# Router logits of a transformer block taken from the un-normed rows, with the row factor, the bias and three small pieces of work moved

## The chip, the core and the metric

The kernel runs on one NeuronCore of one Trainium2 chip. The core has five engines that run their own instruction streams and wait for one another through semaphores: PE (the matrix engine, with its weight loads shown as PEld), DVE (vector work), ACT (activations, casts, copies), POOL (general work and indirect DMA) and SP (which here only issues DMAs). Sixteen DMA engines move data between the chip's memory and the on-chip buffers; SP, ACT and POOL each have a queue that feeds them.

The metric is the device time of one execution in microseconds. The kernel before takes 1404.52 us (median of 3 runs, 1404.02 to 1405.08).

## The reference

One encoder block on a sequence of 1024 rows of width 1024, in float32. Cut to what the change touches:

```python
(shift1, scale1, gate1, shift2, scale2, gate2) = split(silu(c) @ w_ada + b_ada, 6)
...
x  = x + gate1 * (mix @ w_out)                      # mix: two groups of attention heads
h2 = rms_norm(x, norm2_g) * (1 + scale2) + shift2   # rms_norm: x * rsqrt(mean(x*x) + eps) * g
g_logits = h2 @ w_router_group + b_router_group     # 4 groups
e_logits = h2 @ w_router_expert + b_router_expert   # 32 experts, 8 to a group
# the best group; inside it the best 2 experts; weights g_prob * softmax of the two
# each chosen expert: (silu(h2 @ w_gate) * (h2 @ w_up)) @ w_down, width 512 inside
x = x + gate2 * (sum over the two experts, weighted)
return rms_norm(x, final_norm_g)
```

With r = rsqrt(mean(x*x) + eps) of a row, G2 = norm2_g * (1 + scale2) and B2 = shift2, the row is h2 = x * r * G2 + B2, and so h2 @ W + b = r * (x @ (G2 * W)) + (B2 @ W + b).

## The kernel before, in words

The program is one function, `tile_hymba`, written straight down, and a layer under it puts the recorded instructions into one stream per engine. An engine runs its stream strictly in order, so an instruction that waits holds up everything behind it on its engine.

**Stage 1** (to about 260 us) makes the vectors shift1 to gate2 from c, the normed rows, and the projections of the attention heads. Matrix products in float32 are made of three products of a high and a low part (`mm3`, lines 68 to 71). `ada_in`, `ada_add` and `ada_out` interleave the vectors gate1, shift2, scale2 and gate2 (v = 0, 1, 2, 3) with the projections: DVE sums the weighted rows of w_ada into `acc`, and `ada_out(v)` turns `acc` into a column of 128 x 8 on PE (L380), adds the bias on DVE (L382) and stores it to `ada_d` in the chip's memory. When the region of hThi and hTlo is free, SP loads the first heads (L542), and **stage 2**, the attention, follows (to about 640 us).

**Stage 3** (640 to 760 us) is where most of the change lies. It goes over eight tiles t of 128 rows. Per tile: `out_proj` on PE (the tile `pm`, two halves n of 512 columns), `residual(t, n)` on DVE (L972, L973: x2 = pm * gate1 + x) with the sum of squares on ACT, `norm2(t)` (the row factor st[:, 6:7], then h2 = x2 * factor * G2 + B2 in four DVE operations, L992 and L993), the store of h2 to `h2_d` and of x2 to `x2_d`, `flip_h2(t)` (eight transposes on PE, copied out by ACT), and `logits(t)` (eight products with the router's columns `wr`, L1016, and the bias `brt` added on DVE, L1017). The last tile, t = 7, takes its factor by a square root on ACT and a reciprocal; the others by a power on POOL and two Newton steps on DVE (`rsqrt2`).

Two sets of tiles are routed apart: tA (tiles 0 to 4) while stage 3 runs, tB (5 to 7) at its end. `choose` finds group and experts (some 24 small DVE operations), `rank` and `place` give each row its slot, `table` sums one-hot products on PE into `pid` (row numbers) and `pwt` (weights), `weigh` makes the weights in three bfloat16 parts, and `spread` multiplies them out. From `pid` comes `tg`, the table of row numbers; `gather` is an indirect DMA on POOL's queue that reads the rows of an expert from `h2_d`.

**Stage 4** (from 760 us) runs the 32 experts. `x_T` turns the gathered rows (8 transposes, a cast on ACT and a subtraction on DVE for the low part, L1437). The weights, loaded ahead into 14 buffers, are split into high and low parts by `split_e` (a cast on ACT, L1175, and a subtraction on DVE, L1176), one split per chunk of six products on PE. `chunk` asks for splits up to 5 ahead of its own, in program order, so the ten splits before `glu_up` of expert 0 stand ahead of expert 1's `x_T` on DVE. The constants SP0 and SP1 say how many splits are made before the choice and after the gather.

Of the kernel before, what the change touches and what calls it, by code (L numbers as in the profile page):

```python
# [43 lines left out]
SP0, SP1, GU0, NW, NX0 = 2, 3, 13, 14, 4  # L44
# [7 lines left out]
def tile_hymba(  # L52
# [311 lines left out]

    aps = ExitStack()
# [61 lines left out]

    wr = consts.tile([128, 8, 36], F32, name="wr")
    brt = consts.tile([128, 36], F32, name="brt")
    Y.dma_start(wr[:, :, 0:4], w_router_group[0].rearrange("(k p) n -> p k n", p=128))  # L430
    Y.dma_start(wr[:, :, 4:36], w_router_expert[0].rearrange("(k p) n -> p k n", p=128))
    Y.dma_start(brt[:, 0:4], b_router_group.to_broadcast([128, 4]))
    Y.dma_start(brt[:, 4:36], b_router_expert.to_broadcast([128, 32]))
# [531 lines left out]
    def residual(t, n):  # L965

        if n == 0:
            x2s[t] = tile_a(F32)
            sts[t] = sp.tile([128, 8], F32, name="st3", tag="st3", bufs=3)
        ns = slice(n * 512, n * 512 + 512)  # L970
        x2 = x2s[t][:, ns]
        V.tensor_mul(x2, pms[t, n], gate1[:, ns])  # L972
        V.tensor_add(x2, x2, xt3[t][:, ns])  # L973
        A.activation(xt3[t][:, ns], x2, AF.Square, accum_out=sts[t][:, n:n + 1])
        if t == NT - 1 and n == 0:
            A.activation(sts[t][:, 4:5], epsc, AF.Sqrt)
        if t == NT - 1 and n == 1:
            V.tensor_scalar(sts[t][:, 2:3], sts[t][:, 0:1], 1.0 / D, EPS, op0=ALU.mult, op1=ALU.add)
        if n == 1:
            Y.dma_start(x2_d[t * 128:(t + 1) * 128], x2s[t])  # L980

    def norm2(t):
        st = sts[t]
        if t == NT - 1:
            A.activation(st[:, 3:4], st[:, 1:2], AF.Sqrt, bias=st[:, 2:3], scale=1.0 / D)
            V.reciprocal(st[:, 6:7], st[:, 3:4])
        else:
            rsqrt2(st)
# [5 lines left out]
        Y.dma_start(h2_d[t * 128:(t + 1) * 128], h2s[t])  # L994
# [9 lines left out]
    def flip_h2(t):  # L1004
        hTs3[t] = tile_a(F32).rearrange("p (k q) -> p k q", k=8)
        for b in range(2):
            ptr = ps3.tile([128, 512], F32, name="ptr3", tag="tr")
            for i in range(4):
                j = 4 * b + i
                T.transpose(ptr[:, i * 128:(i + 1) * 128], h2s[t][:, j * 128:(j + 1) * 128], ident)  # L1010
            A.copy(hTs3[t][:, 4 * b:4 * b + 4], ptr.rearrange("p (k q) -> p k q", k=4))

    def logits(t):
# [3 lines left out]
        V.tensor_add(LG[:, t], pl[:, 0:36], brt)  # L1017
# [160 lines left out]

    LEAD, LEAD1, ES = 5, 3, 28
# [20 lines left out]
    for t in range(NT + 1):  # L1200
# [3 lines left out]
        elif t < NT:  # L1204
            if t == 3:
                flip_h2(1)
# [15 lines left out]
        if 0 < t:  # L1222
            norm2(t - 1)
        if t == NT:
            split_to(SP0)
            weigh(tA, G)
        flips = [0] if t == 2 else [t - 1] if t > 2 else []
        for u in flips:
            flip_h2(u)
# [23 lines left out]
        if t == NT - 1:  # L1253
            residual(t, 1)
# [18 lines left out]
    gather(xb0, tg[:, 0:1])  # L1273
    weigh(tB, V)
    split_to(SP1)
    table(pwt, EW, tB)
# [74 lines left out]
    def flip4(cols):  # L1351
        ptr = ps4.tile([128, 512], F32, name="ptr4", tag="tr")[:, 0:4 * C]
        for i in range(4):
            T.transpose(ptr[:, i * C:(i + 1) * C], cols[i], ident[:C, :C])  # L1354
        return ptr

    def x_cols(xb, b):

        v = xb.rearrange("c (q p j) -> c q j p", p=128, j=2)
        return [v[:, 2 * b + i // 2, i % 2] for i in range(4)]  # L1360

    def wide(t, i):

        return t[:, i * C:i * C + 128]

    def stat(pool, name, n, dtype=F32R):

        t = pool.tile([128, n * C + 128 - C], dtype, name=name) if pool else tile_a(dtype)[:, :n * C + 128 - C]
        G.memset(f32(t[:, n * C:]), 0.0)
        return t  # L1370

# [58 lines left out]
    def x_T(xb):  # L1430
        xTs.reverse()
        xT = xTs[0]
        for b in range(2):
            ptr = flip4(x_cols(xb, b))
            o = [xT[:, (8 * l + 4 * b) * C:(8 * l + 4 * b + 4) * C] for l in range(2)]
            A.copy(o[0], ptr)
            V.tensor_sub(o[1], ptr, f32(o[0]))  # L1437
        return xT

    def chunk(ps, xT, e, ch):  # L1440
# [3 lines left out]
        for k2 in range(2):  # L1444
            k = 2 * (ch % 4) + k2
            mm3(ps, wide(xT, k), wide(xT, 8 + k), hi[:, k2], lo[:, k2], k == 0, k == 7)
# [6 lines left out]
    xT = x_T(xb0)  # L1453
# [179 lines left out]
```

## Time and profile before

| what | value |
|---|---|
| runs | 1404.52 us median, 1404.02 to 1405.08 |
| the profiled execution | 1404.29 us, its span 1402.5 us |
| PE busy | 1304.8 us, 93% |
| DVE busy | 1082.4 us, 77% |
| ACT busy | 771.9 us, 55% |
| POOL busy | 537.5 us, 38% |
| DMA in all | 357.06 MB, mean 255 GB/s |

The page's strip of 40 slices (35 us each) has one hole in PE's row that this change is near:

```profile
PE   5799999887999999989995999999999989999993
...
PEclk9899999998999999999995999999999999999995
```

Each digit is a busy share in tenths, and PEclk the granted clock of PE in tenths of full speed. Slice 21 (736 to 771 us) is the hand-over from stage 3 to stage 4: PE is at five tenths there and its clock too. Span and execution differ by 1.79 us, which lies around the span.

### The profile page before, as it was taken

How to read it: one execution, taken by the hardware profiler on the slowest of the kernel's cores; microseconds unless marked ns; L12 is line 12 of the kernel's file. 1: busy time of each engine (PE TensorE's matmuls, PEld its weight loads, DVE VectorE, ACT ScalarE, POOL GpSimd, SP SyncE). 2: the span in 40 equal slices, each digit the busy share in tenths (PEclk: the TensorE clock that was granted, in tenths of full speed). 3: DMA queues.
4: the chain of work that ended last, by engine and by line, in shares of the span. 5: the costliest groups of instructions: out<-in, count | busy, mean ns of one | idle time of the engine just before them, and what ended most of it. 6: DMA issues, size and time to landing. Idle time of an engine off the chain costs nothing. (4 is left out here: it accounts for less than half of the span.)

```text
span 1402.5 us, 18267 instructions
## 1 busy us (share of the span) xinstructions
PE 1304.8 (93%) x6343; PEld 1050.9 (75%) x6343; DVE 1082.4 (77%) x1610; ACT 771.9 (55%) x1194; POOL 537.5 (38%) x361
## 2 busy tenths in 40 slices
PE   5799999887999999989995999999999989999993
PEld 4578789765888888878884777777777767777762
DVE  5887646557788888874568798888888888888876
ACT  5531224346666766661224667766666756666653
POOL 2102100047666666650002244444444532544332
PEclk9899999998999999999995999999999999999995
DMA  9528963681344525238966999999989997999946
GB/s 330 163 91 265 309 234 123 182 306 53 87 139 113 172 84 192 71 132 291 342 229 256 357 367 361 356 380 372 324 318 329 354 342 286 363 375 356 380 153 246
DMA packets 123969, 357.06 MB, mean 255 GB/s; under 512 B 15781, under 2 KB 41474, under 8 KB 122338
## 3 DMA queue, kind: packets, MB, share of 16 engines
q1 hardware_dynamic: 79794, 200.11, 41.1%
q10 hardware_dynamic: 29376, 113.25, 21.2%
q0 software_dynamic: 14704, 42.51, 10.0%
q8 instruction: 51, 0.84, 0.2%
q14 instruction: 44, 0.36, 0.1%
HBM read 306.52 MB, written 57.69 MB: 260 GB/s over the span
## 5 line engine op out<-in xcount | busy, mean ns | idle before, releaser
L1176 DVE TENSOR_TENSOR ra<-rb,ra 128x1024 fp32r<-128x1024 f32 x249 | 290.5, 1220 | 51.5 <-ACT ra L1175 47.3
L1348 POOL DMA_INDIRECT x_d<-y,tg x32 | 223.4, 6983 | 124.0 <-DVE y L1418 108.5
L1175 ACT CAST ra<-rb 128x1024 fp32r<-128x1024 f32 x249 | 242.4, 1049 | 1.9 <-PE pg L70 1.3
L626 PE MATMUL s<-ra 128*128 128x512 f32 x448 | 130.8, 409 | 5.1 <-DVE stg L592 3.1
L1176 DVE TENSOR_TENSOR ra<-rx,ra 128x1024 fp32r<-128x1024 f32 x103 | 120.5, 1217 | 17.0 <-ACT ra L1175 14.6
L647 ACT ACTIVATE e<-s,mx 128x1024 f32<-128x1024 f32 x96 | 107.5, 1120 | 38.4 <-DVE mx L642 21.5
L642 DVE TENSOR_REDUCE mx<-s 128x1 f32<-128x1024 f32 x96 | 116.7, 1217 | 12.4 <-PE s L626 12.3
L69 PE MATMUL pz<-whi,hThi 128*128 128x512 f32 (+2 forms) x320 | 118.6, 371 | 5.1 <-ACT hThi L272 5.1
L70 PE MATMUL pz<-wlo,hThi 128*128 128x512 f32 (+2 forms) x320 | 116.5, 364 | 0.4 <-DVE wlo L135 0.4
L69 PE MATMUL pg<-ra,xT 128*128 128x512 f32 x256 | 114.9, 449 | 0.1
L953 POOL DMA_INDIRECT xb<-h_d,tg x31 | 31.0, 999 | 219.1 <-PE ptr L1354 198.7
L71 PE MATMUL pz<-whi,hTlo 128*128 128x512 f32 (+2 forms) x320 | 112.8, 360 | 0.1
L70 PE MATMUL pg<-ra,xT 128*128 128x512 f32 x256 | 102.3, 400 | 6.9 <-DVE ra L1176 6.9
L658 ACT CAST rb<-ptr 128x512 fp32r<-128x512 f32 x128 | 74.3, 588 | 59.8 <-PE ptr L654 59.1
L69 PE MATMUL pu<-ra,xT 128*128 128x512 f32 x256 | 104.1, 407 | 0.0
L71 PE MATMUL pg<-ra,xT 128*128 128x512 f32 x256 | 102.9, 402 | 1.1 <-DVE xT L1437 1.1
L1175 ACT CAST ra<-rx 128x1024 fp32r<-128x1024 f32 x103 | 101.2, 1048 | 2.3 <-DVE ra L1176 1.4
L70 PE MATMUL pu<-ra,xT 128*128 128x512 f32 x256 | 101.1, 395 | 0.1
L71 PE MATMUL pu<-ra,xT 128*128 128x512 f32 x256 | 101.2, 395 | 0.0
L626 PEld LDWEIGHTS s<-ra 128*128 128x128 f32 x448 | 81.6, 191 | 22.8 <-ACT e L647 4.2
L659 DVE TENSOR_TENSOR rb<-ptr,rb 128x512 fp32r<-128x512 f32 x128 | 86.3, 680 | 9.7 <-ACT rb L658 9.5
L654 PE MATMUL ptr<-ident,e 128*128 128x128 f32 x512 | 78.0, 275 | 9.0 <-POOL e L802 5.3
(365 smaller groups left out, 3020.9 us busy)
## 6 DMA issues: line engine op xcount, KB each, us to landing
rb<-in_w_expert_up_dram ACTq DMA_DIRECT2D x26, 1024.0 KB
rb<-in_w_expert_down_dram ACTq DMA_DIRECT2D x26, 1024.0 KB
rb<-in_w_expert_gate_dram ACTq DMA_DIRECT2D x24, 1024.0 KB
rb<-in_w_expert_gate_dram SPq DMA_DIRECT2D x20, 1024.0 KB
rb<-in_w_expert_down_dram SPq DMA_DIRECT2D x20, 1024.0 KB
rb<-in_w_expert_up_dram SPq DMA_DIRECT2D x19, 1024.0 KB
aw<-in_w_ada_dram SPq DMA_DIRECT2D x32, 512.0 KB
ra<-qk_d SPq DMA_DIRECT2D x48, 256.0 KB
```

Of the source, the lines that this page charges most:

```text
L69: T.matmul(ps, ahi, bhi, start=first, stop=False)
L70: T.matmul(ps, ahi, blo, start=False, stop=False)
L71: T.matmul(ps, alo, bhi, start=False, stop=last)
L626: T.matmul(ps[:, ns], l, r[:, ns], start=i == 0, stop=i == len(parts) - 1)
L642: V.reduce_max(mx, ps, axis=AX.X, negate=True)
L647: A.activation(e, ps, AF.Exp, bias=nb, scale=1.0, accum_out=z)
L654: T.transpose(ptr[:, i * 128:(i + 1) * 128], e[:, (4 * b + i) * 128:(4 * b + i + 1) * 128], ident)
L658: A.copy(hi[:, :, q], src)
L659: return lambda: V.tensor_sub(lo[:, :, q], src, f32(hi[:, :, q]))
L1175: A.copy(hi, raw[:, 2 * half:2 * half + 2])
L1176: V.tensor_sub(lo, raw[:, 2 * half:2 * half + 2], f32(hi))
L1348: G.indirect_dma_start(out=x2_d, out_offset=bass.IndirectOffsetOnAxis(ap=si, axis=0), in_=y, in_offset=None, bounds_check=S - 1, oob_is_er ...
```

## The change

It has seven parts.

1. The router's columns and bias are loaded a few lines further up. In `ada_out(1)` the bias becomes brt + shift2 @ W (eight products of 128 x 36 on PE, one DVE addition), and in `ada_out(2)` the columns are multiplied by G2 (one small load, one transpose, two DVE operations).
2. `flip_h2` becomes `flip_x2`: it turns x2, not h2, and `logits` multiplies by the row factor as it adds the bias. For tile 7 the turn comes in two halves, each behind its half of the residual.
3. The stores of h2 are issued from POOL's queue in place of SP's.
4. `weigh(tA)` moves from behind `norm2(7)` to a place ahead of `residual(7, 0)`, and its last multiplication from POOL to DVE.
5. Tile 7 takes its factor by `rsqrt2` as the others do; its h2 is x2 * G2 made in the residual and finished by one operation of 128 x 1024 on DVE behind `choose(tB)`, stored after it.
6. SP0 goes from 2 to 1 and that split moves behind the gather; the turn of expert 0's rows moves ahead of the weights' sum and the positions, with 2 splits behind it.
7. The buffers of the gathered rows are cleared by DVE in place of POOL; the first, `xb0`, is cleared on POOL in tile 7.

```diff
-SP0, SP1, GU0, NW, NX0 = 2, 3, 13, 14, 4
+SP0, SP1, GU0, NW, NX0 = 1, 3, 13, 14, 4
...
+        if v == 1:
+            for k in range(8):
+                T.matmul(pr[:, 256:292], col[:, k:k + 1].to_broadcast([128, 128]), wr[:, k], start=k == 0, stop=k == 7)
+            V.tensor_add(brt, brt, pr[:, 256:292])
+        if v == 2:
+            n2r = ap.tile([8, 128], F32, name="n2r", tag="row8")
+            Y.dma_start(n2r, norm2_g[0].rearrange("(j p) -> j p", p=128))
+            T.transpose(pr[:, 256:264], n2r, ident[:8, :8])
+            V.scalar_tensor_tensor(col, col, 1.0, pr[:, 256:264], op0=ALU.add, op1=ALU.mult)
+            V.tensor_mul(wr, wr, col[:, :, None].to_broadcast([128, 8, 36]))
...
-        G.memset(xbufs[-1], 0.0)
+        V.memset(xbufs[-1], 0.0)
...
-        if t == NT - 1 and n == 0:
-            A.activation(sts[t][:, 4:5], epsc, AF.Sqrt)
-        if t == NT - 1 and n == 1:
-            V.tensor_scalar(sts[t][:, 2:3], sts[t][:, 0:1], 1.0 / D, EPS, op0=ALU.mult, op1=ALU.add)
+        if t == NT - 1:
+            if n == 0:
+                h2s[t] = tile_a(F32)
+            V.tensor_mul(h2s[t][:, ns], x2, G2[:, ns])
...
-        Y.dma_start(h2_d[t * 128:(t + 1) * 128], h2s[t])
+        G.dma_start(h2_d[t * 128:(t + 1) * 128], h2s[t])
...
-                T.transpose(ptr[:, i * 128:(i + 1) * 128], h2s[t][:, j * 128:(j + 1) * 128], ident)
+                T.transpose(ptr[:, i * 128:(i + 1) * 128], x2s[t][:, j * 128:(j + 1) * 128], ident)
...
-        V.tensor_add(LG[:, t], pl[:, 0:36], brt)
+        V.scalar_tensor_tensor(LG[:, t], pl[:, 0:36], sts[t][:, 6:7], brt, op0=ALU.mult, op1=ALU.add)
...
-        if 0 < t:
+        if t == NT:
+            flip_x2(t - 1, [1])
+            rsqrt2(sts[t - 1])
+        elif 0 < t:
             norm2(t - 1)
-        if t == NT:
-            split_to(SP0)
-            weigh(tA, G)
+        if t == NT - 1:
+            weigh(tA, V)
...
             if t == NT - 1:
                 load_w(GU0)
+                flip_x2(t, [0])
...
         if t == NT - 1:
+            xb0 = tile_a(F32)[:C]
+            G.memset(xb0, 0.0)
+        if t == NT - 1:
             residual(t, 1)
...
-    xb0 = tile_a(F32)[:C]
-    G.memset(xb0, 0.0)
     pid, pwt = (pmp.tile([128, 512], F32, name="pt3", tag="pm") for _ in range(2))
     table(pid, EI, tA)
-    table(pwt, EW, tA)
     choose(tB)
+    t = NT - 1
+    V.scalar_tensor_tensor(h2s[t], h2s[t], sts[t][:, 6:7], B2, op0=ALU.mult, op1=ALU.add)
+    G.dma_start(h2_d[t * 128:(t + 1) * 128], h2s[t])
     pcB = rank(tB)
...
     gather(xb0, tg[:, 0:1])
+    table(pwt, EW, tA)
     weigh(tB, V)
+    table(pwt, EW, tB)
+    split_to(SP0)
+    xT0 = [stat(None, "", 8) for l in range(2)]
+    x_turn(xb0, lambda: ps3.tile([128, 512], F32, name="ptr3", tag="tr"), lambda l, b: xT0[l][:, 4 * b * C:(4 * b + 4) * C])
     split_to(SP1)
-    table(pwt, EW, tB)
     V.tensor_copy(wt, pwt[:C, 0:NE])
...
-    xT = x_T(xb0)
+    xT = xT0
```

DVE at the end of tile 6 and in tile 7, before the change: `ra<-pm,ra` is the residual's first operation (pm is out_proj's result), `oc`, `RK` and `ra<-iot_s,RK` are `place(tA)`.

```order
L993 TENSOR_TENSOR ra<-ra,B_6106 128x512
L972 TENSOR_TENSOR ra<-pm,ra 128x512
L973 TENSOR_TENSOR ra<-ra 128x512
L1077 TENSOR_TENSOR oc<-OH,pc 128x320
L1079 TENSOR_REDUCE RK<-oc 128x10
L1081 TENSOR_TENSOR ra<-iot_s,RK 128x960
L972 TENSOR_TENSOR ra<-pm,ra 128x512
L973 TENSOR_TENSOR ra<-ra 128x512
```

The same place after the change; the rows from `w_6880` on are the end of `weigh(tA)`.

```order
L1002 TENSOR_TENSOR ra<-ra,B_6120 128x512
...
L1122 CAST w_6880<-rest 128x10
L1081 TENSOR_TENSOR ra<-OH,w_6880 128x960
L985 TENSOR_TENSOR ra<-pm,ra 128x512
L986 TENSOR_TENSOR ra<-ra 128x512
L991 TENSOR_TENSOR ra<-ra,G_6122 128x512
L1088 TENSOR_TENSOR oc<-OH,pc 128x320
L1090 TENSOR_REDUCE RK<-oc 128x10
L1092 TENSOR_TENSOR ra<-iot_s,RK 128x960
L985 TENSOR_TENSOR ra<-pm,ra 128x512
```

Between norm2(6) and residual(7, 0) now stand the ten operations of `weigh(tA)`, and a multiplication by G2 stands behind each half of the residual.

DVE from the gathered rows of expert 0 to those of expert 1, before: `xT<-ptr` is the low part of the turned rows, `ra<-rx,ra` and `ra<-rb,ra` are splits of weights, `sg<-sg,pu` is `glu_up`.

```order
L1282 COPY cnt<-pc 128x32
L1437 TENSOR_TENSOR xT_7118<-ptr_7129,xT_7118 128x384
L1437 TENSOR_TENSOR xT_7118<-ptr_7136,xT_7118 128x384
L1176 TENSOR_TENSOR ra<-rx,ra 128x1024 x5
L1176 TENSOR_TENSOR ra<-rb,ra 128x1024 x5
L1378 TENSOR_TENSOR sg<-sg,pu 96x512
L1437 TENSOR_TENSOR xT_7116<-ptr_7252,xT_7116 128x384
```

The same stretch after:

```order
L1216 TENSOR_TENSOR ra<-ptr_7088,ra 128x384
L1216 TENSOR_TENSOR ra<-ptr_7095,ra 128x384
L1187 TENSOR_TENSOR ra<-rx,ra 128x1024 x2
L1329 COPY wt<-pt_6971 96x32
...
L1334 COPY cnt<-pc 128x32
L963 MEMSET xb_7136 96x1024
L963 MEMSET xb_7138 96x1024
L1187 TENSOR_TENSOR ra<-rx,ra 128x1024 x5
L1187 TENSOR_TENSOR ra<-rb,ra 128x1024 x5
L1409 TENSOR_TENSOR sg<-sg,pu 96x512
L1216 TENSOR_TENSOR xT_7151<-ptr_7271,xT_7151 128x384
```

Two splits, the sum of the weights with the positions (`wt` to `cnt`) and two clearings now stand between the two turns; before, only the ten splits and `glu_up` did.

## Rows read from the trace of the kernel before

**Rows 1.** The page's first line.

```profile
span 1402.5 us, 18267 instructions
```

**Rows 2.** Windows: stretch, length, busy us of engines, PEclk, DMA share, GB/s.

```profile
740.00:745.00 5.00, 4.70 (x24) 4.33 (x23) 4.42 (x12) 2.46 (x3) 0.17 (x1) 0.50 1.03 421
755.00:760.00 5.00, 0.47 (x7) 0.47 (x6) 4.82 (x7) 0.00 (x0) 3.13 (x5) 0.50 0.21 63
800.00:840.00 40.00, 40.00 (x182) 31.52 (x181) 35.21 (x38) 26.31 (x34) 21.00 (x5) 1.00 1.01 368
```

**Rows 3.** Waits of PE, 770 to 1375 us: total, times, longest.

```profile
PE pg L70 <- DVE ra L1176: 6.9, 1, 6.9
```

**Rows 4.** Waits of SP's queue, 150 to 300 us.

```profile
SPq L542 <- PE pz L71: 29.4, 1, 29.4
```

**Rows 5.** Timeline of DVE, the last two tiles: start, us, operation.

```profile
730.21 0.69 DVE L993 TENSOR_TENSOR ra<-ra,B 128x512 f32<-128x512 f32 x1
731.45 0.69 DVE L972 TENSOR_TENSOR ra<-pm,ra 128x512 f32<-128x512 f32 x1 [0.55 <-PE pm L71]
...
733.82 1.16 DVE L1081 TENSOR_TENSOR ra<-iot_s,RK 128x960 bf16<-128x960 f32 x1
735.06 0.69 DVE L972 TENSOR_TENSOR ra<-pm,ra 128x512 f32<-128x512 f32 x1
```

**Rows 6.** The same: weigh(tA), first and last of nine, then the choice.

```profile
742.85 0.17 DVE L1103 TENSOR_REDUCE gs<-GE 128x5 f32<-128x20 f32 x1
...
744.52 0.18 DVE L1111 CAST w<-rest 128x10 bf16<-128x10 f32 x1
745.19 0.19 DVE L1017 TENSOR_TENSOR LG<-pl,brt 128x36 f32<-128x36 f32 x1 [0.49 <-PE pl L1016]
...
745.62 1.03 DVE L1028 TENSOR_TENSOR fk<-LG,GM 128x12 f32<-128x12 f32 x1
```

**Rows 7.** Timeline of PE, end of stage 3 to the first expert.

```profile
734.87 1.87 PE L1016 MATMUL pl<-wr,ra 128*128 128x36 f32 x16
739.42 1.09 PE L1010 MATMUL ptr<-ident,ra 128*128 128x128 f32 x4 [2.69 <-DVE ra L993]
...
741.69 3.47 PE L1016 MATMUL pl<-wr,ra 128*128 128x36 f32 x16
...
759.97 1.51 PE L1354 MATMUL ptr<-ident,ra 96*128 96x96 f32 x8
...
```

**Rows 8.** Timeline of DVE from the choice's end to expert 1's rows.

```profile
750.65 0.26 DVE L1050 TENSOR_TENSOR OB<-OH 128x96 bf16<-128x96 f32 x1
...
754.04 0.18 DVE L1272 TENSOR_TENSOR tg<-tgf,pt 96x32 int32<-96x32 f32 x1
...
755.42 2.85 DVE L1111 CAST w<-rest 128x6 bf16<-128x6 f32 x1
...
760.53 0.18 DVE L1277 COPY wt<-pt 96x32 f32<-96x32 f32 x1
...
763.04 0.18 DVE L1282 COPY cnt<-pc 128x32 f32<-128x32 f32 x1
...
764.08 5.75 DVE L1176 TENSOR_TENSOR ra<-rx,ra 128x1024 fp32r<-128x1024 f32 x5
...
778.13 1.01 DVE L1437 TENSOR_TENSOR xT<-ptr,xT 128x384 fp32r<-128x384 f32 x2
```

**Rows 9.** Timeline of POOL: the first gather and a clearing.

```profile
755.10 1.14 POOL L953 DMA_INDIRECT ra<-h_d,tg  x1 [7.59 <-DVE wts L1106]
756.25 0.97 POOL L950 MEMSET xb<- 96x1024 f32 x1
```

**Rows 10.** The tile qk_d: landing of POOL's 256 KB stores in stage 1.

```profile
DMA to landing us min/median/max: 2.3/4.1/10.1
```

**Rows 11.** The lines with DVE's clearings: durations in ns, first start, form.

```profile
L79 DVE MEMSET ones<- x1: 165/165/165, 0.9 to 0.9; 128x128 f32 x1
L81 DVE MEMSET epsc<- x1: 59/59/59, 1.0 to 1.0; 128x1 f32 x1
```

More of the change, by code (lines that the diff above doesn't have):

```diff
@@ L362, in tile_hymba @@
         V.tensor_copy(nlam, plam[:, 0:1])
+    wr = consts.tile([128, 8, 36], F32, name="wr")
+    brt = consts.tile([128, 36], F32, name="brt")
+    Y.dma_start(wr[:, :, 0:4], w_router_group[0].rearrange("(k p) n -> p k n", p=128))
+    Y.dma_start(wr[:, :, 4:36], w_router_expert[0].rearrange("(k p) n -> p k n", p=128))
+    Y.dma_start(brt[:, 0:4], b_router_group.to_broadcast([128, 4]))
+    Y.dma_start(brt[:, 4:36], b_router_expert.to_broadcast([128, 32]))
     aps = ExitStack()
@@ L425, in tile_hymba @@
                 turn_pair(rps, h, sb.tile([128, 2, 512], F32R, name="stg", tag="stg", bufs=4), hs, 2)
[L428 to L433, printed above, removed]
     iot = consts.tile([128, 48], F32, name="iot")
@@ L983, in norm2 @@
         st = sts[t]
[L984 to L988, printed above, removed]
+        rsqrt2(st)
         h2s[t] = tile_a(F32)
@@ L1002, in rsqrt2, with flip_x2 @@
         V.tensor_mul(st[:, 6:7], st[:, 5:6], st[:, 4:5])
-    def flip_h2(t):
-        hTs3[t] = tile_a(F32).rearrange("p (k q) -> p k q", k=8)
-        for b in range(2):
+    def flip_x2(t, bs=range(2)):
+        if t not in hTs3:
+            hTs3[t] = tile_a(F32).rearrange("p (k q) -> p k q", k=8)
+        for b in bs:
             ptr = ps3.tile([128, 512], F32, name="ptr3", tag="tr")
@@ L1177, in split_e, with flip4, x_cols, wide @@
         return hi, lo
+    def flip4(cols, new=None):
+        ptr = (new() if new else ps4.tile([128, 512], F32, name="ptr4", tag="tr"))[:, 0:4 * C]
+        for i in range(4):
+            T.transpose(ptr[:, i * C:(i + 1) * C], cols[i], ident[:C, :C])
+        return ptr
+    def x_cols(xb, b):
+        v = xb.rearrange("c (q p j) -> c q j p", p=128, j=2)
+        return [v[:, 2 * b + i // 2, i % 2] for i in range(4)]
+    def wide(t, i):
+        return t[:, i * C:i * C + 128]
+    def stat(pool, name, n, dtype=F32R):
+        t = pool.tile([128, n * C + 128 - C], dtype, name=name) if pool else tile_a(dtype)[:, :n * C + 128 - C]
+        G.memset(f32(t[:, n * C:]), 0.0)
+        return t
+    def x_turn(xb, new, part):
+        for b in range(2):
+            ptr = flip4(x_cols(xb, b), new)
+            A.copy(part(0, b), ptr)
+            V.tensor_sub(part(1, b), ptr, f32(part(0, b)))
     LEAD, LEAD1, ES = 5, 3, 28
@@ L1205, in tile_hymba @@
             if t == 3:
-                flip_h2(1)
+                flip_x2(1)
             if t < NT - 1:
@@ L1221, in tile_hymba @@
             load_w(GU1)
-        if 0 < t:
+        if t == NT:
+            flip_x2(t - 1, [1])
+            rsqrt2(sts[t - 1])
+        elif 0 < t:
             norm2(t - 1)
-        if t == NT:
-            split_to(SP0)
-            weigh(tA, G)
+        if t == NT - 1:
+            weigh(tA, V)
         flips = [0] if t == 2 else [t - 1] if t > 2 else []
         for u in flips:
-            flip_h2(u)
+            if t < NT:
+                flip_x2(u)
         if 0 < t < NT:
@@ L1349, in scatter @@
                              in_=y, in_offset=None, bounds_check=S - 1, oob_is_err=False, compute_op=ALU.add)
[L1351 to L1370, printed above, removed]
     def glu_gate(pg):
@@ L1432, in x_T @@
         xT = xTs[0]
[L1433 to L1438, printed above, removed]
+        x_turn(xb, None, lambda l, b: xT[:, (8 * l + 4 * b) * C:(8 * l + 4 * b + 4) * C])
+        return [xT[:, 0:8 * C + 128 - C], xT[:, 8 * C:]]
     def chunk(ps, xT, e, ch):
```

2 lines of the change are left out of this document (1 added, 1 removed).

## The prediction

> **What bounds the kernel now.** I read the span first [rows 1], then the windows by stage, then PE's waits, then the timelines of PE, DVE and POOL round the hand-over from stage 3 to the experts, because the parts of the change lie there and in stage 1. In the expert stage PE is busy in all of a 40 us window at the full clock [rows 2], and in 600 us it waits once for longer than 2.2 us, 6.9 us for a split of DVE [rows 3]. So that stage is a fixed length of PE work, and what counts is when PE gets expert 0's and expert 1's rows and whether splits arrive in time. At the hand-over PE is idle most of the time and its clock is at 0.50, 1.2 GHz, where it is at 1.00, 2.4 GHz, in the experts [rows 2]; the reader is to see DVE at 4.4 and 4.8 of 5 us there: it sets the pace. DMA is saturated at 740 to 745 and at 0.21 at 755 to 760 [rows 2]: the loads ahead are in by then.
>
> **The change, part by part.**
>
> *Stage 1.* Eight more products of PE. Eight products with the 36 columns of `wr` take 1.87 us at the full clock [rows 7]; I take 1.8. They lie on the path: SP's first loads for the attention wait for PE's last product of this stage, 29.4 us in all [rows 4], and everything later follows from those. The transpose and the three DVE operations are small beside it and DVE waits for PE there. Bounds: 0, if a later wait for something else swallows it, and 2.0.
>
> *Un-normed rows and POOL's stores, tiles 0 to 6.* PE is the busy engine until 735 us and does as many transposes and products as before; the multiplication is in the same DVE operation as the bias. SP no longer waits for h2 between its loads, but PE does not wait for those loads. The stores stand on POOL between the factors' powers, each behind the h2 of its own tile, which is finished long before the next power is asked for. I cost all this at nothing; the cover is PE's full queue, and without it each store would put its issue before a power.
>
> *weigh(tA) ahead of residual(7, 0).* DVE finishes norm2(6) at 730.21 + 0.69 = 730.90 and then waits 0.55 for PE [rows 5]: that is all the room there is. The nine small operations take 742.85 to 744.70, 1.85 us [rows 6]; the multiplication that comes over from POOL has 960 columns and I take the 1.16 of place's operation of that size [rows 5]. So residual(7, 0) starts at 733.91 and not 731.45. From there to the end of place it was 734.98 - 731.45 = 3.53, and the G2 operation adds 0.69: residual(7, 1) starts at 738.13 in place of 735.06 [rows 5], 3.1 us late.
>
> A cast of the second weigh took 2.85 us and not 0.18 [rows 6, 8], while POOL issued the gather and cleared buffers from 755.10 on [rows 9]. After the change three such casts run at 731.7 to 732.8, just when POOL issues the store of h2(6) and then clears `xb0` (0.97 [rows 9]). The stall there lies between 0 and the 1.0 of that clearing; I take 0.5. The Trainium skill, "SBUF — State Buffer", section "Who interferes with whom", says that a cast of DVE can use two ports and then shares a lock with POOL, so that whoever comes second waits for all of the other's instruction. By it the stall would be the whole 1.0 and the sum 0.5 us more. The same page warns of DMAs issued from POOL for the mirror reason; no row here has DVE's casts holding up an issue.
>
> *The last tile.* x2's second half is there 1.4 us after 738.6, at 740.0. Before, its normed rows reached PE in two parts at 739.42 and 740.8, PE's clock low after an idle of 2.69 us, and the eight products took 3.47 us from 741.69, against 1.87 at the full clock [rows 7]. Now one half is turned already; the other takes 1.09 at the low clock, the products start at about 741.0 and the logits are there at 744.55 and not 745.19 [rows 6]. The factor is ready earlier: its chain is 1.8 us behind the sum of squares. So four DVE passes saved buy only 0.65 us, since DVE came 3.6 us late. If PE held 2.4 GHz through 740 us, half of 1.09 + 3.47 would go, and the logits come at 742.3.
>
> *Choice to gather.* It was 745.19 to 754.22, 9.03 us [rows 6, 8]. One operation there took 1.03 and its neighbours 0.18, beside POOL's part of weigh, which is gone: -0.85. The last h2 operation of 128 x 1024 is inserted, 1.15 (five in 5.75 [rows 8]). Row numbers at 744.55 + 9.33 = 753.9, before 754.2. The gather started 0.9 after that [rows 9]. Now it also waits for the last store, which cannot be issued before 744.55 + (750.91 - 745.19) - 0.85 + 1.15 = 750.6. Landing: 256 KB stores of POOL took 2.3 to 10.1, median 4.1 [rows 10]; this one has 512 KB but quieter engines than at 740. I take 4.1: 754.7, and the gather at 754.8 in place of 755.10. With 2.3 the 0.9 could go too; with 10.1 the gather starts at 760.7. Expert 0's rows are turned 4.87 us behind the gather's start [rows 7, 9], so the hand-over moves by -0.3 (bounds -3 and +5.6).
>
> *Expert 0 to expert 1.* Call the start of that turn F, 759.97 before [rows 7]. Then DVE had 18.16 us until the low part of expert 1's rows at 778.13 [rows 8], and PE had finished expert 0 by then. Now DVE has, in this order: 1.5 for PE's turn [rows 7], 1.0 for two subtractions, 2.3 for two splits, 2.6 from `wt` to `cnt` (760.53 to 763.15), two clearings, 11.5 for ten splits, 0.6 for `glu_up`. For the clearings the only rows of DVE are 165 ns for 128 columns and 59 ns for one [rows 11]: 0.83 ns a column, 0.9 for 1024 columns (bounds 0.17, if the size hardly counts, and POOL's 0.97). That is F + 21.3, 3.15 late. Before, the two splits lay at 740 us, in front of the choice, the sum of the weights lay beside PE's first turn, and the clearings were POOL's. This is the largest term, and no later slack gives it back, since PE's work from expert 1 on is a fixed length. Bounds: 1.5, clearings cheap and the misses partly in DVE's own old gaps, and 4.
>
> *The clock.* PE idles some 3 us there, and after 2.69 us it was found at half clock [rows 7]. Some products at 1.2 GHz, between 0 and 2 us; I take 0.5.
>
> Sum: 1.8 - 0.3 + 3.15 + 0.5 = 5.15. Against the profiled execution's own 1404.29, which is its span and 1.79 around it and lies 0.2 below the median of the runs: 1404.29 + 5.15 = 1409.4.
>
> **Rivals.**
>
> *The clock holds.* The turn of the first half and tile 6's logits now fill PE's gap after 735 us. If that keeps PE at 2.4 GHz to the choice, the logits come at 742.3, the store is out by 748.4, and the hand-over moves by -0.3 - 2.25; expert 1 then has no clock to lose. It decides if the clock falls later than 741. For it: one gap of 2.7 us becomes two short ones. Against it: 0.50 in all of 740 to 745 [rows 2], and the second gap is still some 2 us. 1.8 - 2.55 + 3.15 = +2.4: 1406.7, not slower by what can be told.
>
> *The late work of DVE is hidden.* If ACT or the buffers hold the ten splits back, as a gap of 2 us in DVE's row between them did before, the extra 3.15 lies in time that was lost anyway. With the hand-over as in the clock's case and stage 1's products swallowed by the attention's waits: 0 - 2.55 - 0.5 (the gather earlier by most of its 0.9) = -3: 1401.3, faster. Against it: the ten splits stand behind the clearings in one stream, ACT's casts are ahead by then.
>
> *The last store is late.* The gather waits for all eight h2 stores. If POOL's store shares the engines with the last weights, it lands like the 10.1 us row, and the hand-over is 5.6 late: 1409.4 + 5.9 = 1415.3. Against it: 0.21 of DMA at 755 [rows 2].
>
> **How the numbers follow.** Forecast 0.52, the clock holds 0.22, hidden 0.14, late store 0.12. About 0.2% (2.8 us) is what a measurement of this kernel can tell from no change. The forecast's own range, 1406 to 1412, is slower by 0.2% in about nine of ten: 0.47 slower, 0.05 same. The clock's case lies on the edge: 0.17 same, 0.03 slower, 0.02 faster. Hidden: 0.09 faster, 0.05 same. Late store: slower. Together slower 0.62, same 0.27, faster 0.11. The range, with both outer cases cut to 2 in 10: 1402.5 to 1412.5.
>
> **What would show it.** In the profile after: PE's last product of stage 1 at about 1.8 us later; residual(7, 1) 3 us later than that against its old place; the logits of tile 7 near their old time; the gather waiting for a DMA or for the row numbers; DVE without a gap from expert 0's turn to expert 1's and PE waiting some 3 us at expert 1's first low-part product. I am wrong if the stage 1 shift is gone by 640 us, if PE does not wait at expert 1, or if the clock stands at 1.00 through 745 us.

## The result: 1.3% slower, most of it one gather that stood on POOL

| | median us | runs |
|---|---|---|
| before | 1404.27 | 1401.16 to 1405.08, 4 runs |
| changed | 1421.83 | 1419.98 to 1422.56, 4 runs |

The ratio is 1.0126 with a 95% interval of 1.0114 to 1.0139. The prediction said 1409.4 with a range to 1412.5: the direction was right and the size was not, 17.6 us in place of 5.

The page's first line and two rows of its strip, in the changed kernel (slices of 35.5 us):

```profile
span 1420.5 us, 18319 instructions
...
PE   5799999897999999989995699999999989999993
...
PEclk9899999999999999999996899999999999999996
```

The hole at the hand-over now spreads into the slice behind it. The windows (columns as in [rows 2]) show both halves of it, the old one at 740 to 760 us and a new one at 785 to 795, where PE is busy 1.48 of 10 us; from 800 us on PE is full again as before:

```profile
740.00:745.00 5.00, 3.10 (x24) 3.04 (x25) 4.86 (x9) 2.01 (x5) 0.00 (x0) 0.75 1.03 421
755.00:760.00 5.00, 1.51 (x16) 1.43 (x17) 3.73 (x16) 1.10 (x3) 1.52 (x2) 0.50 0.26 105
785.00:795.00 10.00, 1.48 (x8) 1.26 (x8) 0.45 (x2) 0.48 (x1) 2.50 (x3) 0.60 1.03 316
800.00:840.00 40.00, 40.00 (x182) 31.52 (x181) 32.72 (x36) 25.52 (x34) 15.70 (x4) 1.00 0.92 318
```

PE's waits from 770 to 1375 us, to be read against [rows 3], name it. The 6.9 us wait is still there; above it stands a new one for `xb`, the gathered rows of expert 1, and it is a wait for a DMA, not for DVE:

```profile
PE ptr L1193 <- DMA xb<-h_d,tg: 11.8, 1, 11.8
PE pg L70 <- DVE ra L1187: 9.5, 2, 6.9
```

POOL's timeline round the hand-over shows why the DMA was late. L966 is the gather, L1311 the store of the last h2:

```profile
755.04 0.59 POOL L1311 DMA_DIRECT2D h_d<-ra  x1 [9.09 <-DVE EM L1106]
759.07 1.08 POOL L966 DMA_INDIRECT ra<-h_d,tg  x1 [3.44 <-DVE w L1122]
...
773.82 11.88 POOL L966 DMA_INDIRECT xb<-h_d,tg  x1 [2.34 <-DVE xb L963]
785.70 0.81 POOL L1170 DMA_DIRECT2D rb<-in_w_expert_up_dram  x1
```

Expert 0's gather took 1.08 us on POOL, expert 1's 11.88. Before, the latter stood ahead of the splits:

```profile
764.00 0.99 POOL L953 DMA_INDIRECT xb<-h_d,tg  x1 [0.69 <-POOL hF L1369]
```

DVE's timeline beside it (to compare with [rows 5], [rows 6] and [rows 8]):

```profile
735.42 1.16 DVE L1122 CAST w<-wts 128x10 bf16<-128x10 f32 x1
...
738.52 0.68 DVE L985 TENSOR_TENSOR ra<-pm,ra 128x512 f32<-128x512 f32 x1
...
748.62 0.26 DVE L1028 SCALAR_TENSOR_TENSOR LG<-pl,st,brt 128x36 f32<-128x36 f32 x1 [1.99 <-PE pl L1027]
...
757.81 0.18 DVE L1319 TENSOR_TENSOR tg<-tgf,pt 96x32 int32<-96x32 f32 x1
...
772.63 0.91 DVE L963 MEMSET xb<- 96x1024 f32 x1 [0.16 <-issue]
773.47 5.69 DVE L1187 TENSOR_TENSOR ra<-rx,ra 128x1024 fp32r<-128x1024 f32 x5
779.08 5.76 DVE L1187 TENSOR_TENSOR ra<-rb,ra 128x1024 fp32r<-128x1024 f32 x5
784.76 0.68 DVE L1409 TENSOR_TENSOR sg<-sg,pu 96x512 f32<-96x512 f32 x1
794.98 1.20 DVE L1216 TENSOR_TENSOR xT<-ptr,xT 128x384 fp32r<-128x384 f32 x2 [9.55 <-ACT xT L1215]
```

The gather was asked for at 773.82, inside the first of ten splits that follow one another without a gap, and it ended at 785.70, which is 0.94 behind the start of `glu_up` at 784.76: its own work (0.96 where nothing holds it) done once the splits were over. DVE then idled 9.55 us, and PE started expert 1 at 795.00 in place of 777.97.

The hold is not all of the delay. The rows landed 19.6 us after the gather was asked for:

```profile
DMA to landing us min/median/max: 19.6/19.6/19.6
```

Of these 11.9 are POOL's, and 7.8 passed behind them, at a DMA share of 1.03 in 785 to 795. Expert 0's rows landed 3.1 us behind their gather's end, at a quieter time. How much sooner the rows would have come through free DMA engines was not tested.

Four markers cut the 18.0 us between the two spans into stretches:

| marker | before | changed | lost in the stretch |
|---|---|---|---|
| PE, last `prb` turn of the attention | 632.22 | 635.97 | 3.75 |
| PE, turn of expert 0's rows | 759.97 | 763.40 | -0.32 |
| DVE, low part of expert 1's rows | 778.13 | 794.98 | 13.42 |
| end of the span | 1402.5 | 1420.5 | 1.15 |

The first and the last line are single readings. The attention's end moves by some us among the profiles of the same stage 1 (below), and the last stretch is 623.9 to 627.7 us long in the profiles of the experiments that change nothing in it, against 624.4 before and 625.5 here.

### The profile page after: what moved, and what is told of

Read it like the earlier page. It is cut to its first block, busy times and chain, and to the rows that moved or that the text cites. A ratio compares the mean times of both kernels' runs of the same rounds, so it can differ in the third digit from the quotient of the medians.

```text
span 1420.5 us, 18319 instructions
## 1 busy us (share of the span) xinstructions
PE 1305.5 (92%) x6360; PEld 1050.5 (74%) x6360; DVE 1085.2 (76%) x1618; ACT 768.7 (54%) x1190; POOL 548.8 (39%) x369
## 5 line engine op out<-in xcount | busy, mean ns | idle before, releaser
L966 POOL DMA_INDIRECT xb<-h_d,tg x31 | 41.7, 1346 | 218.4 <-PE ptr L1193 196.4
L69 PE MATMUL pg<-ra,xT 128*128 128x512 f32 x248 | 111.0, 447 | 0.0
L70 PE MATMUL pg<-ra,xT 128*128 128x512 f32 x248 | 98.6, 398 | 6.9 <-DVE ra L1187 6.9
L69 PE MATMUL pu<-ra,xT 128*128 128x512 f32 x248 | 101.0, 407 | 0.0
L71 PE MATMUL pg<-ra,xT 128*128 128x512 f32 x248 | 98.8, 398 | 0.0
L71 PE MATMUL pu<-ra,xT 128*128 128x512 f32 x248 | 98.2, 396 | 0.0
L70 PE MATMUL pu<-ra,xT 128*128 128x512 f32 x248 | 98.0, 395 | 0.1
```

The source lines that it names most:

```text
L69: T.matmul(ps, ahi, bhi, start=first, stop=False)
L70: T.matmul(ps, ahi, blo, start=False, stop=False)
L71: T.matmul(ps, alo, bhi, start=False, stop=last)
```

## The experiments

### The gather that is held

`e1_clear_on_pool`, the clearings back on POOL:

```
-        V.memset(xbufs[-1], 0.0)
+        G.memset(xbufs[-1], 0.0)
```

> The changed kernel with one edit: the two buffers of the gathered rows are cleared by POOL again. The trace of the changed kernel has expert 1's gather on POOL for 11.88 us, from 773.82 to 785.70, beside ten splits of DVE that follow one another without a gap from 773.47 to 784.84. Theory A (DVE's run of splits keeps POOL from writing the gather's descriptors): the gather still stands on POOL behind the clearing of hF, which waits for DVE's positions, so it is asked for just when the splits begin; it starts some 2 us earlier and is again held for about 11 us, to the end of the splits. PE waits about 10 us for expert 1's rows; 1419.5 to 1420.5, some 2 us under the changed kernel. Theory B (the gather was late because it stood behind the two clearings on DVE): it takes about 1 us, its rows land before DVE has done the splits, and PE waits about 3 us; some 9 us under the changed kernel, 1412 to 1414.

Measured: 1411.50 us, 1.0048 [1.0031, 1.0065] of before, some 10 us under the changed kernel. The number is near theory B's 1412 to 1414, the trace is neither's:

```profile
772.81 0.12 POOL L1208 MEMSET hF<- 128x32 f32 x1 [0.38 <-DVE pos L1134]
773.57 1.28 POOL L966 DMA_INDIRECT xb<-h_d,tg  x1 [0.63 <-POOL hF L1208]
774.85 0.81 POOL L1170 DMA_DIRECT2D rb<-in_w_expert_up_dram  x1
```

The gather is asked for in the first of the ten splits here too (they began at 772.77), and the second began at 773.90: 773.90 + 0.95 is the gather's end. It got in at the first boundary between two splits. So theory A was right that a split holds the gather, and wrong that a run of splits always holds it to its end.

`e2_gather_early`, the clearings on POOL and the gather ahead of the small clearings of `xTs` and `hs4`:

```
+    for i in range(1, NX):
+        x_in(i)
     xTs = [stat(xp, "xT%d" % i, 16) for i in range(2)]
     hs4 = stat(xp, "hT", 2 * DS), stat(xp, "hF", 4 - DS, F32)
-    for i in range(1, NX):
-        x_in(i)
```

> As the run before, and expert 1's gather moves ahead of the four small clearings on POOL, so that POOL issues it right behind the clearing of its buffer, near 762 us, while DVE waits for PE's turn. Theory A (the run of splits holds the gather): it takes about 1 us, its rows are there by 771, and PE waits at expert 1 for DVE alone, until the splits, glu_up and the two subtractions of expert 1's rows are done near 784.5; 10 us off the changed kernel, 1411 to 1413, which is what is left of the predicted terms (3.7 from stage 1 and 3 to 4 for DVE's backlog). Theory B (clearings): no more than in the run before. Theory C (the DMA engines are full of weights then, and the rows land late whenever they are asked for): the rows land after 785 and PE waits 5 us or more for them.

Measured: 1411.47 us, 1.0049 [1.0032, 1.0065]; the gather at 765.34, 1.41 long, its rows there 4.5 us after it was asked for, and no wait of PE for it. The same time as the run before: once the rows are there in time, earlier buys nothing. PE then waits 2.5 us for DVE's low part, near the 3 of the prediction:

```profile
PE pg L71 <- DVE xT L1216: 2.5, 1, 2.5
```

Theory C falls, since rows asked for in time land in time.

`e3_small_op_between`, an addition of 128 x 1 behind every split:

```
         V.tensor_sub(lo, raw[:, 2 * half:2 * half + 2], f32(hi))
+        V.tensor_add(dot, dot, dot)
```

> The changed kernel with a DVE addition of 128 x 1 behind every split, which touches nothing else. In the traces POOL's scatters take 7.85 us while DVE goes from split to split and 1.44 where DVE is idle. Theory A1 (whatever ends the run of splits lets POOL in, a small operation too): scatters of 2 to 3 us, expert 1's gather done by 777 and PE's wait for it 3 us in place of 11.8; about 8 us less. Theory A2 (DVE keeps the right of way as long as its next operation is of the kind that needs it, whatever its size): scatters stay at 7 to 8 us, and the gather is held until the last of the ten splits and takes 12 to 13 us; the time is the changed kernel's or 1 us more.

Measured: 1413.49 us, one run, some 8 us under the changed kernel as theory A1 had it. POOL's timeline, two gathers and a scatter:

```profile
773.88 1.66 POOL L966 DMA_INDIRECT xb<-h_d,tg  x1 [2.34 <-DVE xb L963]
...
776.65 9.74 POOL L966 DMA_INDIRECT xb<-h_d,tg  x1 [0.30 <-issue]
...
807.69 8.28 POOL L1403 DMA_INDIRECT x_d<-y,tg  x1 [3.16 <-DVE y L1452]
```

A mixed answer. The first gather got in at the first boundary; the second, expert 2's, was held past fourteen boundaries of splits and small additions, to the last addition ahead of `glu_up` (785.44 + 0.95) or to `glu_up` itself, which starts 0.07 later; the scatters stay at 8.0 to 8.3 through most of the experts, as theory A2 had it. A small operation of the same kind (both inputs on chip) does not open the way by itself.

`f3_short_run`, six splits in place of ten in that run:

```
-        split_to(at + 1 + (LEAD if e < ES else LEAD1))
+        split_to(at + 1 + (1 if e == 0 else LEAD if e < ES else LEAD1))
```

> The changed kernel with one number: in expert 0 splits are asked for one chunk ahead in place of five, so that six and not ten splits stand between the two clearings and glu_up. The clearings stay on DVE. Theory (the run of splits holds the gather, to its end or to a boundary that it happens to get): the gather takes at most 7.8 us, PE's wait for its rows falls from 11.8 to 7 or less, and the time is 4 to 9 us under the changed kernel, 1413 to 1418. Rival (it is late by the clearings ahead of it, or by the queue of its DMAs): it takes 10 to 12 us again and the time stays at 1421.

Measured: 1412.03 us, 1.0053 [1.0037, 1.0069]; the gather, still behind DVE's two clearings, took 1.66 us (first boundary), and PE waited 0.3 us for its rows:

```profile
772.71 1.66 POOL L966 DMA_INDIRECT xb<-h_d,tg  x1 [2.34 <-DVE xb L963]
```

```profile
PE ptr L1193 <- DMA xb<-h_d,tg: 0.3, 1, 0.3
```

Less than the range expected, and the rival falls: with the clearings where they are in the changed kernel, 9.8 us go when the gather is not held. The edit also takes four splits out of DVE's way, so the 9.8 are not the hold's alone; `e1_clear_on_pool` and `e2_gather_early` keep all ten splits and agree (10.3 and 10.4).

`g1_changed_again`, `g2_clear_a_column` and `g3_clear_half`: the changed kernel as it is, and with one line ahead of the gather (1 and 512 columns):

```
+    G.memset(xbufs[1 % NX][:, 0:1], 0.0)
     for i in range(1, NX):
         x_in(i)
```

> The changed kernel once more, unchanged, beside the two below. If which boundary between two splits lets the gather in is settled by the program's own timing, expert 1's gather takes 11.9 us again, and PE waits 11.8 for its rows; 1420 to 1422.5. If it is chance from one execution to the next, the gather takes some other one of the values that end a split, and the time lies between 1411 and 1422.

> The changed kernel with one more clearing on POOL, of one column of expert 1's buffer, between DVE's clearing of it and its gather, so that the gather is asked for 0.1 to 0.4 us later in the first split and nothing else moves. If the moment of asking decides: the gather takes another time than 11.9 (1 to 8 us) and PE's wait changes with it. If it does not: 11.5 again.

> The same with 512 columns, some 0.5 us of POOL. If POOL's clearing needs the same right of way as its descriptors, it is the clearing that waits for a boundary and the gather follows it without a wait (1.0 us). If only the descriptors do, the clearing takes 0.5 beside the split and the gather waits for a boundary, the next or a later one.

Measured: 1420.06, 1422.51 and 1420.04 us (two runs each). Of the first the gather, of the second and the third the added clearing and the gather, in this order:

```profile
772.91 11.88 POOL L966 DMA_INDIRECT xb<-h_d,tg  x1 [2.33 <-DVE xb L963]
```

```profile
773.89 0.10 POOL L1477 MEMSET xb<- 96x1 f32 x1 [2.12 <-DVE xb L963]
774.64 11.34 POOL L966 DMA_INDIRECT xb<-h_d,tg  x1 [0.66 <-POOL xb L1477]
```

```profile
773.09 0.52 POOL L1477 MEMSET xb<- 96x512 f32 x1 [2.12 <-DVE xb L963]
773.89 6.75 POOL L966 DMA_INDIRECT xb<-h_d,tg  x1 [0.28 <-POOL xb L1477]
780.65 0.81 POOL L1170 DMA_DIRECT2D rb<-in_w_expert_up_dram  x1
```

The changed kernel repeats its 11.88 to the digit, which speaks against chance. Asked for 0.5 us later in the first split (0.89 into it in place of 0.35), the gather ends at the same boundary, `glu_up`; behind half a clearing it got in at the start of the seventh split (779.70 + 0.95). The clearing itself ran beside the split in 0.52, unhindered, and so did the plain DMA behind the gather (0.81). What decides which boundary a gather gets is not settled by these runs. In every one of these three and in the changed kernel a held gather ended 0.94 to 0.96 behind the start of one of DVE's operations.

### Stage 1

`e4_no_bias_products` leaves the eight products of shift2 with the router's columns out, and the addition that reads them (the rows are then routed otherwise, so its time, 1413.99 us in one run, is not compared); `f2_before_products` is the other way round, the kernel before with eight such products that nothing reads:

```
+        if v == 1:
+            for k in range(8):
+                T.matmul(pr[:, 256:292], col[:, k:k + 1].to_broadcast([128, 128]), ident[:, 0:36], start=k == 0, stop=k == 7)
```

> The changed kernel without the eight products of the shift with the router's columns in stage 1 (so the logits lack that part, the routing differs, and the time is read only up to 735 us). By the trace PE is 1.0 us late ahead of them, 2.7 behind them, and 3.7 at the last out_proj. If the products are the cost: 1.7 to 2 us of the 3.7 go, and some 1.8 stay (the small transpose and other orders of waiting). If the attention has waits that would absorb or restore a shift of this size: the end of the attention stands where it is, 3.7 late or 0.

> The kernel before with one addition: eight products of 128 x 36 on PE in the second of the four vectors, with nothing reading their sum. It is the PE part of the change's stage 1 alone. Theory: they lie on PE's path to the end of stage 1 and cost 1.9 us or, with the waits of DVE and PE behind them that they shift, about 3 as between the changed kernel and the run without its products: 1407.3. Rival: the difference of 3 us at 632 us between those two runs is the spread of the attention's start from run to run; then the time is within 1 us of before.

Measured: the marker at the attention's end, in `e4_no_bias_products` and then in `f2_before_products` (635.97 in the changed kernel, 632.22 before):

```profile
632.82 0.60 PE L737 MATMUL prb<-ident,r 128*128 128x128 f32 x4
```

```profile
635.48 0.60 PE L729 MATMUL prb<-ident,r 128*128 128x128 f32 x4
```

Without the products 3.15 of the 3.75 go; with them alone 3.26 come. `f2_before_products` takes 1407.05 us, 1.0024 [1.0015, 1.0033] of before, 3.4 us, so all of it reaches the end. The products themselves are the 1.87 expected. Behind them PE's wait for a tile of the attention's preparation grows by 1.0, from 3.1 before to this in `f2_before_products`:

```profile
PE s L629 <- DVE stg L595: 4.1, 1, 4.1
```

The last 0.4 is not accounted for. In the changed kernel itself the wait for that tile takes another form, 1.4 and, for an earlier product, 2.0. One caution: in the profiled executions of the other runs that hold the change's stage 1 as it is, the marker lies between 634.95 and 638.84, 2.7 to 6.6 late, though the work up to there is the same. The 3.75, and the 3.15 and 3.26 beside it, are single readings that are good to a microsecond or two; the firm number is the 3.4 us of the whole, from 11 runs against 23.

`e7_products_late`, the products, the bias and the scaling behind the last vector:

```
-        if v == 1:
+        if v == 3:
             for k in range(8):
-                T.matmul(pr[:, 256:292], col[:, k:k + 1].to_broadcast([128, 128]), wr[:, k], start=k == 0, stop=k == 7)
+                T.matmul(pr[:, 256:292], cols[1][:, k:k + 1].to_broadcast([128, 128]), wr[:, k], start=k == 0, stop=k == 7)
```

> The first experiment with the eight products, the bias and the scaling of the router's columns behind the last of the four vectors in place of the second and the third, so that they stand at the start of the attention's preparation, where PE waits 4.1 us for DVE in one place. Theory: they lie in that wait; PE is 1 us late at 632 us in place of 3.7 to 5.3, and the time is 2 to 3 us less, 1409. Rival: they are still ahead of the products that DVE waits for, and nothing changes.

Measured: 1414.87 us, 1.0079 [1.0062, 1.0096], slower than the first experiment. The products ran at 259.59 and took 3.29 there, and the marker is at 638.34. By the marker no wait hid them, though a low clock blurs the reading. They cost more because PE's clock fell in this profile: the granted clock was 0.50, 1.2 GHz, in 260 to 264, where it was 1.00 in the kernel before, the changed kernel and the first experiment, and 1.00 in 255 to 260 with PE busy in all of it.

```profile
260.00:264.00 4.00, 4.00 (x21) 4.00 (x20) 2.25 (x8) 0.00 (x0) 0.34 (x1) 0.50 1.04 254
```

That gives 1.4 of the 3.4 us between the two experiments; why the clock fell, and the rest, are left open.

### The hand-over and the order behind the choice

`e5_weigh_back`, the first experiment with `weigh(tA)` at its old place and its multiplication on POOL:

```
             rsqrt2(sts[t - 1])
+            weigh(tA, G)
         elif 0 < t:
             norm2(t - 1)
-        if t == NT - 1:
-            weigh(tA, V)
```

> The first experiment (clearings on POOL, 1411.5 us) with weigh(tA) back behind the factor of tile 7 and its last multiplication on POOL. Theory: the ten operations ahead of residual(7, 0), 4.0 us with the cast that stood 1.16 beside POOL, made DVE late for the last tile; their removal brings residual(7, 0) to PE's half of tile 7 (DVE waits 0.5 for PE again), the logits come 3 us earlier, and in their new place they lie in DVE's wait of 2 us for the logits; an operation of the choice is held 0.85 by POOL's multiplication. 2 to 3 us less than the first experiment: 1409. Rival: the clock of PE falls the same and DVE's next 8 us to the choice are a chain through PE and POOL in which 4 us of DVE change little: within 1 us.

Measured: 1409.26 us, 1.0037 [1.0024, 1.0050]. The interval overlaps the first experiment's; between the markers at the attention's end and at the turn of expert 0's rows the stretch falls from 127.40 to 125.54 us, and that is the clearer evidence for some 1.9: the profiles with `weigh(tA)` at its new place have 127.1 to 128.2 there, and `f4_after_mended`, which has it back too, 125.44 (`e8_three_undone`, which has the old order of `e6_order_back` as well, 128.98). DVE's timeline shows what was won and what came back, a wait for PE at residual(7, 0) and an operation of the choice beside POOL's multiplication:

```profile
737.01 0.69 DVE L985 TENSOR_TENSOR ra<-pm,ra 128x512 f32<-128x512 f32 x1 [0.62 <-PE pm L71]
...
747.30 1.66 DVE L1039 TENSOR_TENSOR fk<-LG,GM 128x12 f32<-128x12 f32 x1
```

`e6_order_back`, the first experiment with SP0 = 2 ahead of the choice, and weights' sum, positions and one split ahead of the turn (the move of the turn is not shown):

```
-SP0, SP1, GU0, NW, NX0 = 1, 3, 13, 14, 4
+SP0, SP1, GU0, NW, NX0 = 2, 3, 13, 14, 4
...
             rsqrt2(sts[t - 1])
+            split_to(SP0)
```

> The first experiment with the order behind the choice as it was: a second split ahead of the choice, and weights' sum, positions and one split ahead of the turn of expert 0's rows. Theory: this gives back the term of 3.15 that the prediction had for DVE's backlog before expert 1 (the wait of 2.4 for the low part of its rows and the splits that came late), and the split costs nothing where DVE waits 2 us for the logits: 3 us less, 1408.5. It also brings the gather of expert 1 ahead of the ten splits, where it takes 1.0 to 1.3. Rival: the early turn of expert 0's rows had gained what the later wait lost: no change.

Measured: 1410.71 us, 1.0047 [1.0031, 1.0064]: no change that can be told from the first experiment. The rival held. Expert 0's first product now comes 3.8 us behind the turn (763.43 to 767.21) where in the first experiment it was 2.1 (764.88 to 766.95), and PE waits 2.27 of it for DVE's low part of the turn. At expert 1 PE's wait for the low part falls from 2.4 to 0.8: what the old order gains there it loses here.

`e8_three_undone`, the edits of `e5_weigh_back`, `e6_order_back` and `e7_products_late` together:

> The first experiment with the three edits of the runs beside this one together. If the terms add: 7 to 8.5 us less, 1403 to 1404.5, no slower than the kernel before; what is left of the change is then the un-normed rows, the stores on POOL and the late finish of the last h2. If they overlap (one wait behind the other): 1406 to 1408.

Measured: 1413.67 us, 1.0056 [1.0039, 1.0072], single runs from 1407.7 to 1415.1. That is outside both forecasts. They do not add, as the third cost time by itself and the second gained none; inconclusive as to the rest.

`f4_after_mended`: the clearings on ACT, the early gather and `weigh(tA)` at its old place:

> The changed kernel with three edits: the clearings on ACT, expert 1's gather right behind its clearing, and weigh(tA) back behind the factor of tile 7. If the terms add up: the experiment with weigh(tA) back had 1409.3 with the clearings on POOL, where casts of DVE stood 2.6 us beside them; without that stall 1407 to 1408.5, which leaves the 3 to 5 us of stage 1 and the attention's start as the change's net cost, and stage 3 with stage 4 equal to those of the kernel before.

Measured: 1409.67 us, 1.0045 [1.0030, 1.0060], outside the expected 1407 to 1408.5 and no better than `e5_weigh_back`. What stays is 6.0 us, more than the 3 to 5 forecast, and the products give 3.4 of it. By the markers of its profile against those of the kernel before, the attention ends 3.9 late, the stretch to the turn of expert 0's rows is 2.3 shorter (125.44 for 127.75), the low part of expert 1's rows comes 1.7 later behind that turn, and the last stretch is 2.1 longer. So stage 3 is the faster one once `weigh(tA)` is back, and stage 4 gives it up again; these are single readings, and no run takes the last two apart.

### A version that beats both

`f1_before_clear_act`, the kernel before with the clearings on ACT and the gather of `e2_gather_early`:

```
-        G.memset(xbufs[-1], 0.0)
+        A.activation(xbufs[-1].rearrange("c (a b) -> c a b", b=128), ones[:C, None, :].to_broadcast([C, 8, 128]), AF.Copy, scale=0.0)
```

> The kernel before with one step changed: the two buffers of the gathered rows are cleared by ACT, idle from 752 to 760 us there, in place of POOL, and expert 1's gather is issued right behind its buffer's clearing. In the trace of before a cast of DVE stands 2.85 us beside POOL's gather and clearings (755.42 to 758.27), and PE later waits 1.12 for the low part of expert 0's rows. Theory: the cast takes 0.2 to 1.0 without the clearings, DVE reaches that low part 1 to 2 us earlier, PE's wait of 1.12 goes and the splits of expert 0 begin earlier: 1 to 2 us faster than before, 1402.5 to 1403.5. Rival: PE is at 1.2 GHz there and the splits are asked for later anyway: no change. Second rival: the ten splits now begin ahead of a gather and hold it, as in the changed kernel: slower by some us.

Measured: 1401.63 us against 1403.63, 0.9987 [0.9978, 0.9995]. That is a gain of 0.1%, small but clear of the noise. The cast of 2.85 us [rows 8] takes 0.39, and expert 1's rows have their low part at 775.76 and not 778.13; the two edits were not run apart:

```profile
755.75 0.39 DVE L1111 CAST w<-rest 128x6 bf16<-128x6 f32 x1
...
760.96 1.20 DVE L1437 TENSOR_TENSOR xT<-ptr,xT 128x384 fp32r<-128x384 f32 x2 [0.28 <-ACT xT L1436]
...
775.76 1.01 DVE L1437 TENSOR_TENSOR xT<-ptr,xT 128x384 fp32r<-128x384 f32 x2
```

## Why the prediction was wrong, step by step

**Stage 1** was mis-sized: 1.8, bounds 0 to 2.0, measured 3.75 in the trace and 3.4 for the products alone. The product group was priced right (1.87); the upper bound assumed that a delay on the path costs its own length at most, and in `f2_before_products`, which has the products alone, a wait behind them grew by 1.0 more.

**Tiles 0 to 6 at nothing** held: PE's last out_proj is 3.81 late, what stage 1 had cost.

**weigh(tA)** held, with the larger end of its stall. The cast took 1.16 where its neighbours take 0.18, beside POOL's store and clearing: 1.0 and not 0.5. The Trainium skill's rule ("SBUF — State Buffer", "Who interferes with whom"), that the later one waits for all of the other's instruction, gave that size. Which of the two came first the rows leave open: the cast's begins at 735.42, 0.14 ahead of the clearing's.

**The last tile and the choice** held: taken against the 3.75, the logits are 0.3 early (0.65 said); logits to row numbers took 9.37 us (9.33 said); the gather began at 759.07, 4.0 behind the asking for the last store (755.04), where 4.2 was said. The hand-over moved by -0.32 (-0.3 said). That both agree so closely is in part luck. The store landed after 3.0 us and not 4.1, at 758.02, with the row numbers (757.99); the gather began 1.05 behind both and not 0.1; and the turn came 4.33 behind the gather's start and not 4.87.

**Expert 0 to expert 1** is the step that failed: "That is F + 21.3, 3.15 late", where 13.42 was measured. The DVE row itself came out: `glu_up` ended at F + 22.0. What the step left out is the DMA. It followed the two clearings only as DVE time and not the gather that waits for them. That gather came to stand in the run of ten splits, its rows landed at F + 30, and PE waited 11.8 us. The run with the clearings on POOL shows the step without that: F + 19.8 for the low part, 1.7 late, where the prediction's own list without the two clearings gives F + 19.5. So the sum of DVE's work was right, and what was wrong is that DVE alone sets the time.

The prediction dismissed the warning with the sentence "no row here has DVE's casts holding up an issue". For casts that is so, but DVE's subtractions hold up scatters, which are issued on POOL as the gathers are. Of the 32 scatters of the kernel before 29 take 5.5 to 7.9 us and three 1.4 to 2.3. Two from POOL's timeline, and the splits beside the first:

```profile
798.09 7.93 POOL L1348 DMA_INDIRECT x_d<-y,tg  x1 [3.09 <-DVE y L1418]
...
1147.27 1.44 POOL L1348 DMA_INDIRECT x_d<-y,tg  x1 [3.08 <-DVE y L1418]
```

```profile
797.73 5.75 DVE L1176 TENSOR_TENSOR ra<-rb,ra 128x1024 fp32r<-128x1024 f32 x5
803.40 1.22 DVE L1176 TENSOR_TENSOR ra<-rx,ra 128x1024 fp32r<-128x1024 f32 x1
804.54 0.45 DVE L1388 TENSOR_TENSOR hT<-ptr,hT 128x288 fp32r<-128x288 f32 x1
```

The scatter of 7.93 ends at 806.02, 1.48 behind the first operation of DVE that follows the splits; the one of 1.44 fell into a time when DVE was idle. The same instruction at two lengths, the longer one ending with a run on another engine, points to something that both need, and it was there to be read. The prediction looked only for casts, and at the first gather.

**The clock**: 0.5 said. PE began expert 1 after an idle of 11.85 us with the granted clock at 0.60 in 785 to 795, and the start of its ninth product there came 2.93 us behind that of the first, where it was 2.26 before: 0.7 lost. The 1.15 from expert 1's low part to the end can't all be put down to it, since that stretch varies by more.

**The rivals**: none of them happened, and none of the four cases has the gather of expert 1 in it. The direction, slower, came out for a reason that the forecast did not have, though stage 1 and DVE's list would have given some of it: with the gather not held the kernel was still 0.5% slower (`e1_clear_on_pool`). The late store needed 10 us to land and took 3.0; the clock fell (0.75 in 740 to 745, 0.50 in 755 to 760); the backlog was not hidden.

## What to carry to other kernels

When an operation moves to another engine, follow what waits for it, DMAs above all, to the place where that is issued now, and ask what the other engines do at that moment. A row whose duration varies for the same shape (1.44 and 7.93) prices a contention without any experiment: look for the shortest and the longest before saying that there is none. A delay on the path is priced by its length only as long as the waits behind it stay the same, so the upper bound lies above it.

## What the runs showed of the hardware

- An indirect DMA on POOL (which reads its row numbers from the chip's buffer) is held by DVE's two-input operations whose inputs both lie there (the splits), and can miss several boundaries between them: five in `g3_clear_half`, nine in the changed kernel. A hold that lasted to an operation that reads PSUM (`glu_up`, `hT`) ended there: the gather 0.94 behind the start of `glu_up`, 25 of the 32 scatters before 1.39 to 1.48 behind that of `hT`. The plain DMA of a weight took 0.78 to 0.81 beside the same splits and a clearing on POOL 0.52. The Trainium skill ("SBUF — State Buffer", "Who interferes with whom") says that a two-input operation of DVE contends with a POOL instruction that reads the buffer and not with one that only writes; these rows agree. It says too that the holder keeps it for the instruction; here the hold went from one split to the next without letting go.
- Clearing 96 x 1024 takes 0.91 us on DVE, 0.97 on POOL and 1.0 on ACT; beside it on POOL a cast of DVE took 1.0 us longer (one clearing), and 2.7 us longer beside a gather and two clearings.
